# An RWKV/HGRN layer on one core: RWKV in units of four head pairs, HGRN in units of two heads, attention scores of 256 queries a bank

## The chip, the cores and the metric

The kernel runs on one core of a Trainium2 chip. The metric is the device time of one execution in microseconds (us). A core has TensorE (PE, with its weight loads as PEld), VectorE (DVE), ScalarE (ACT), GpSimd (POOL), SyncE (SP, which here issues the transfers) and 16 DMA engines. Matrix products land in the eight banks of PSUM (`bank` in the profile), all else lies in SBUF.

## The reference

One layer works on 1024 prompt tokens and 32 sample tokens of width 1024; the sample has its own recurrent states and memory.

```python
n = rmsnorm(x, norm_mix); p = n @ w_in                 # 2048 HGRN + 1792 RWKV columns
x += concat(hgrn2(p[:, :2048]), rwkv7(p[:, 2048:])) @ w_out
x += cross_attend(rmsnorm(x, norm_cross), mem_k, mem_v, w_cq, w_co)   # 4 heads of 256, 256 memories
n = rmsnorm(x, norm_ffn)
x += (silu(n @ w_ff1) * (n @ w_ff3)) @ w_ff2           # width 2816
y = rmsnorm(x, norm_final)
# hgrn2: 4 heads of 128, state S[k, v]
S = decay[:, None] * S + k_t[:, None] * v_t;  o_t = q_t @ S
# rwkv7: 8 heads of 64, state S[v, k]
sa = S @ (-kk_t)
S = S * w_t + outer(sa, kk_t * a_t) + outer(v_t, k_t); y_t = S @ r_t
```

The outputs are y for both, the last HGRN and RWKV states, the last projected RWKV row, and the memory's keys and values. Inputs and outputs are float32.

## The kernel before

Activations lie with their features on the partitions and the 1056 tokens along the free axis, in blocks of 352 or quarters of 264. A float32 product is made of three fp32r products (high x high, high x low, low x high): each weight tile of 1024 x 128 is loaded (`wr`), cast to its high part by ScalarE (`rw`) and split into its low part by VectorE (`rw<-wr,rw`), and a block of it is 24 dense matmuls (`gemm`, L881; the same in `fast`, L1283, and `memory_kv`, L994). Small products of the mixers go in plain float32, which PE runs as two records each.

The stages, by the profiled execution: mixers and input projection (0 to 708 us), keys and values of the memory (654 to 723), output projection (723 to 840), cross attention (708 to 1117), the two halves of the feed-forward (1079 to 1536 and 1536 to 1749), the last norm (to 1776).

`load_rows` (L905) loads nine tiles of x with 128 tokens (32 in the last), squares them on ScalarE, takes the root on GpSimd, scales by norm and gain on VectorE, transposes on PE and splits into high and low parts (ScalarE casts, VectorE subtracts). The gain comes as a broadcast transfer of 128 x 1024. `keep_rows` (L939) transposes each raw tile and stores it for the residual.

`mixers` (L1506) then writes the mixers' work. Projected tiles go to DRAM (`p_scratch`) and come back in the shape that a unit wants. `first` (L1609) projects r, k and v for the head pairs 0 and 1, six tiles of 128 columns, in the first block of 352 tokens and then in the others; the other tiles come as each consumer is written.

`rwkv(j)` (L1644) is called for the head pairs 0,1 and for 2,3. A unit is two pairs by 256 tokens, as eight chunks of 64 tokens, four units and one of 32 tokens for the sample. Its first half (kind `rw`) makes decays, keys, masked products of a chunk and the inverse of a triangular matrix. Its second half (kind `rc`) walks the chunks in order: a state step is the product `ps_b`, an addition, the product `ps_sa`, two copies, the product `ps_h` and the new state. Each of the three products is four matmuls of 64 columns (two pairs, two halves), and there are 17 steps for each call, 34 in all.

`hgrn(i)` (L1949) handles one head. A unit is 256 tokens of it in two groups of 128: exponentials and logarithms on ScalarE, a scan over blocks of 32 tokens, products of queries and keys with them, a masked 128 x 128 score for each group (`copy_predicated`), the state update, and the normed, gated output. There are four units and a sample unit for each head, 20 in all.

`attend` (L1108) scores 128 queries against 256 memories in a bank, takes maximum, exponential and sum, scales, transposes, splits, and multiplies with the values.

The order is not that of the code. Every operation is recorded as a node (L348) and all are issued at L392, so each row of the profile has that line. `plan` (L462) chooses the order by lists: it goes by each node's rank (the longest way to the end, moved by `START` and `NUDGE`, a table of numbers), by estimated costs (`price`, L229), by how many buffers of a kind are free (`FIFO`, L73), by how many units of a kind may be open, and by a charge for PE to change between forms of its array (`change`, L304). All engines then run their lists in order and wait for each other's semaphores.

## Time and profile before

| | |
|---|---|
| runs | 1792.44, 1788.71, 1786.61 us, median 1788.71 |
| profiled execution | 1785.72 us, its span 1783.9 |
| mean granted clock of TensorE | 0.997 |
| busy, share of the span | PE 98%, PEld 93%, DVE 73%, ACT 49%, POOL 25% |
| instructions | PE 15823, DVE 2743, ACT 2071, POOL 628 |
| the chain that ended last | PE 65%, DVE 8%, ACT 3%, DMA 2% |

A row of the timeline has the start, the duration, the engine, the line, the operation, what it writes and reads with its shape, how many operations the row joins, and in brackets the idle time before it and what ended it. A group of the page has busy time, mean ns of one and the idle time of the engine before them. A row of the table by stretches has the stretch, its length, busy time and count of PE, PEld, DVE, ACT and POOL, the clock granted, the DMA share and GB/s. `f`, `mb`, `r`, `rw`, `rs` and `wr` are kinds of SBUF memory, each shared by many tiles.

### The profile page before, as it was taken

The numbers are of one execution on the slowest core, as the hardware profiler recorded it, in microseconds if no ns is written. First come the engines' busy times: TensorE is split into PE (matmuls) and PEld (weight loads), VectorE is DVE, ScalarE is ACT, GpSimd is POOL, SyncE is SP. The second block draws the span as 40 slices with busy tenths as digits, with TensorE's granted clock in tenths as the row PEclk, the third lists the DMA queues.
The fourth block names the chain that finished last, engine by engine and source line by source line (L and its number), as shares of the span: only waits on it lengthen the run. The fifth ranks groups of instructions, "written<-read, shape, count | busy, mean of one in ns | idle before, by whom it ended". The sixth has DMA issues, their size and how long they took to land.

```text
span 1783.9 us, 40074 instructions
## 1 busy us (share of the span) xinstructions
PE 1741.6 (98%) x15823; PEld 1666.1 (93%) x15823; DVE 1296.0 (73%) x2743; ACT 875.2 (49%) x2071; POOL 448.0 (25%) x628
## 2 busy tenths in 40 slices
PE   7999999999999999999999999999999999999998
PEld 6998988899888889999999999999999999999997
DVE  6467669857876887323755367998877778968997
ACT  5755557664657668432333356332333333653432
POOL 5000112321102314252000047323322223222321
PEclk9999999999999999999999999999999999999999
DMA  7733223242323148642121242133222244655522
GB/s 222 211 106 108 64 80 89 66 118 88 102 57 96 45 131 260 214 145 85 54 78 36 78 147 90 34 125 113 91 99 99 94 131 151 193 151 158 182 84 98
DMA packets 213900, 203.99 MB, mean 114 GB/s; under 512 B 19448, under 2 KB 201072, under 8 KB 213712
## 3 DMA queue, kind: packets, MB, share of 16 engines
q1 hardware_dynamic: 213712, 201.44, 36.4%
q8 instruction: 124, 2.03, 0.5%
q14 instruction: 64, 0.52, 0.1%
HBM read 140.64 MB, written 60.75 MB: 113 GB/s over the span
## 4 chain that ended last, share of the span: by engine, by line
PE 65%; DVE 8%; ACT 3%; DMA 2%; issue 1%; POOL 0%; SPq 0%; DVEq 0%; ACTq 0%
PE bank L392 65%; DVE f L392 3%; DVE mb L392 3%; ACT mb L392 2%; DVE rw L392 1%; DVE r L392 1%; ACT f L392 1%; SPq L392 0%; POOL f L392 0%; DMA f<-mix_scratch 0%; DMA p_scratch<-mb 0%; ACT rw L392 0%; DMA f<-in_w_cv_dram 0%; DMA out_dram<-f 0%; DMA mix_scratch<-f 0%
## 5 line engine op out<-in xcount | busy, mean ns | idle before, releaser
L392 PE MATMUL bank<-r,rw 128*128 128x264 f32 (+1 forms) x5928 | 894.6, 304 | 9.5 <-DVE rw L392 4.6
L392 PEld LDWEIGHTS bank<-r,rw 128*128 128x128 f32 x5928 | 840.1, 188 | 17.9 <-DVE rw L392 6.1
L392 PE MATMUL bank<-mb,rw 128*128 128x264 f32 (+3 forms) x3672 | 514.7, 293 | 1.2 <-DVE f L392 0.6
L392 PEld LDWEIGHTS bank<-mb,rw 128*128 128x128 f32 x3672 | 485.7, 188 | 6.5 <-DVE f L392 1.4
L392 DVE TENSOR_TENSOR f<-bank,f 128x264 f32<-128x264 f32 (+5 forms) x466 | 207.7, 456 | 150.7 <-PE bank L392 135.8
L392 ACT CAST rw<-wr 128x1024 fp32r<-128x1024 f32 (+3 forms) x163 | 117.6, 728 | 192.2 <-PE bank L392 164.1
L392 POOL TENSOR_TENSOR f<-f 128x2 f32<-128x2 f32 (+8 forms) x170 | 104.2, 623 | 333.3 <-ACT f L392 261.6
L392 DVE TENSOR_TENSOR f<-f 128x264 f32<-128x264 f32 (+6 forms) x257 | 167.8, 671 | 18.7 <-ACT f L392 14.1
L392 ACT ACTIVATE f<-f 128x256 f32<-128x256 f32 (+6 forms) x275 | 119.9, 458 | 119.0 <-DVE f L392 74.4
L392 DVE TENSOR_TENSOR rw<-wr,rw 128x1024 fp32r<-128x1024 f32 (+3 forms) x163 | 143.2, 886 | 31.6 <-ACT rw L392 23.2
L392 PE MATMUL bank<-f 128*128 128x128 f32 (+15 forms) x1008 | 146.5, 287 | 2.8 <-DVE f L392 1.0
L392 ACT CAST rw<-r 128x512 fp32r<-128x512 f32 (+2 forms) x123 | 69.2, 564 | 118.7 <-PE bank L392 98.2
L392 PE MATMUL bank<-f,mb 128*128 128x64 f16 (+2 forms) x1969 | 110.0, 217 | 15.4 <-DMA mb<-in_x_prompt_dram 6.7
L392 PEld LDWEIGHTS bank<-f 128*128 128x128 f32 (+7 forms) x1008 | 105.4, 159 | 19.1 <-issue 4.3
L392 ACT COPY mb<-bank 128x512 f32<-128x512 f32 (+5 forms) x175 | 77.1, 453 | 75.1 <-PE bank L392 58.2
L392 DVE TENSOR_TENSOR rw<-r,rw 128x512 fp32r<-128x512 f32 (+2 forms) x123 | 86.9, 708 | 31.0 <-ACT rw L392 30.1
L392 PE MATMUL bank<-mb 64*64 64x64 f32 (+6 forms) x2060 | 94.8, 225 | 3.5 <-DVE mb L392 3.2
L392 ACT COPY f<-bank 128x264 f32<-128x264 f32 (+5 forms) x197 | 67.3, 361 | 61.5 <-PE bank L392 57.5
L392 PEld LDWEIGHTS bank<-mb 64*64 64x64 f32 (+3 forms) x1852 | 69.9, 138 | 15.2 <-issue 4.7
L392 ACT ACTIVATE mb<-mb 128x512 f32<-128x512 f32 (+8 forms) x141 | 75.6, 551 | 10.5 <-POOL mb L392 5.8
L392 PEld LDWEIGHTS bank<-f,mb 64*64 64x64 f32 (+4 forms) x1021 | 53.1, 140 | 22.2 <-issue 9.3
L392 POOL TENSOR_TENSOR r<-r 128x512 f32<-128x512 f32 (+2 forms) x37 | 53.4, 1450 | 79.9 <-DMA r<-in_w_ff_dram 45.9
(166 smaller groups left out, 1829.3 us busy)
## 6 DMA issues: line engine op xcount, KB each, us to landing
wr<-in_w_in_dram SPq DMA_DIRECT2D x36, 512.0 KB
p_scratch<-mb SPq DMA_DIRECT2D x87, 176.0 KB
wr<-in_w_ff_dram SPq DMA_DIRECT2D x26, 512.0 KB
r<-in_w_ff_dram SPq DMA_DIRECT2D x26, 512.0 KB
f<-h_scratch SPq DMA_DIRECT2D x33, 264.0 KB
f<-p_scratch SPq DMA_DIRECT2D x66, 128.0 KB
r<-h_scratch SPq DMA_DIRECT2D x31, 264.0 KB
h_scratch<-f SPq DMA_DIRECT2D x19, 396.0 KB
```

The lines of the kernel that those rows point to most:

```text
L392: getattr(eng, method)(*args, **kw)
```

## The change

- RWKV is one pass: a unit is all four head pairs by 128 tokens, still eight chunks of 64. There are eight units and a sample unit, 17 state steps, each product with eight matmuls. Products with the small weights (`psw`, `psa`, the gate) have 128 columns, and v is transposed earlier. `first` projects all twelve r, k and v tiles for the first block and then for the others.
- HGRN takes two heads at once, 512 columns, in ten units. Operands are written in place of their sources, the clamp goes from GpSimd to VectorE, one `copy_predicated` masks four groups. All HGRN units stand behind RWKV in the code.
- Attention scores, maxima, sums and transposes of 256 queries share a bank, and the products with the values take the term with the low part of the probabilities last.
- `gemm`, `fast` and `memory_kv` issue, for every four tiles of depth, four products high x high, four with the low activations and four with the low weights.
- `load_rows` begins with an activation of one element, loads the gain as one row of 4 KB and spreads it by two matmuls with ones; raw tiles are kept for the residual only behind the tile at token 256.
- The planner knows when within a node an operand is needed (`lag`), charges turns between dense and other work (`TURN`), counts two more GpSimd operations as sharing VectorE's port, and has fewer buffers for `pr` and `ph`, four for `cg`, and another table.

```diff
-START, NUDGE = (68066, 0.2), ((35, 7642, 3), (55, 8846, 3), ...
+START, NUDGE = (94419, 0.1), ((40, 8857, 0.3), (50, 3388, 3), ...
+TURN = 0.035, -0.06, 0.085, 0.0
-FIFO = {..., "pr": 6, "pl": 2, "ph": 12, ...}
+FIFO = {..., "pr": 3, "pl": 2, "ph": 4, ..., "cg": 4}
...
+def lag(n, s):
+    return wait(n, s) - (s.preds[n] or 0.0)
...
# gemm
-                nc.tensor.matmul(ps, lhsT=hi[:, k], rhs=ah, start=i == 0, stop=False)
-                nc.tensor.matmul(ps, lhsT=hi[:, k], rhs=al, start=False, stop=False)
-                nc.tensor.matmul(ps, lhsT=lo[:, k], rhs=ah, start=False, stop=i == nk - 1)
+                for part, w in ((0, hi), (1, hi), (0, lo)):
+                    for k in ks[i:i + CUT]:
+                        nc.tensor.matmul(ps, lhsT=w[:, k], rhs=act(k, part, t0, n), ...
...
# load_rows
+        S.activation(warm[:, 0:1], warm[:, 1:2], AF.Square)
+        row = self.tmp([128, D], "grow1")[0:1]
+        nc.sync.dma_start(row, self.i["norm_mix"]).soon = SOON
-        nc.sync.dma_start(gain, self.i["norm_mix"].to_broadcast([128, D])).soon = SOON
+            PE.matmul(ps, lhsT=self.ones[0:1], rhs=row[:, 512 * kg:512 * kg + 512], start=True, stop=True)
+            V.tensor_copy(gain[:, 512 * kg:512 * kg + 512], ps)
...
# attend
-                    ps = self.psm.tile([128, 256], F32, tag="m", name="ps_sc")
+                ps = self.psm.tile([128, 2, 256], F32, tag="m", name="ps_sc")
-                    V.tensor_reduce(st[:m, 0:1], ps[:m], mybir.AxisListType.X, ALU.max)
+                V.tensor_reduce(st[:m, 0, :ng], ps[:m, :ng], mybir.AxisListType.X, ALU.max)
-                    terms = [(a, x, y) for a in range(2) for x, y in (((0, 0), (0, 1), (1, 0)) ...
+                    terms = [(a, x, y) for x, y in (((0, 0), (1, 0), (0, 1)) ... for a in range(2)]
...
# mixers, first
-        for j in (0, 2):
-            self.rwkv(j)
-            for i in (j, j + 1):
-                self.hgrn(i)
+        self.rwkv()
+        for i in (0, 2):
+            self.hgrn(i)
-            for tile in (0, 1, 4, 5, 8, 9):
+            for tile in range(12):
                 self.rw_proj(tile, bias=0.0, blocks=blocks)
...
# rwkv
-        for s in range(5):
-            m, c0 = (4, 256 * s) if s < 4 else (1, TP)
+        for s in range(9):
+            m, c0 = (2, 128 * s) if s < 8 else (1, TP)
             for c in range(m):
-                ps = self.psc.tile([128, 2, 64], F32, tag="c", name="ps_b")
-                for a in range(2):
+                ps = self.psc.tile([128, 4, 64], F32, tag="c", name="ps_b")
+                for a in range(4):
...
# hgrn
-            G.tensor_scalar(e, f, -80.0, 3e38, ALU.max, ALU.min)
+            V.tensor_scalar(e, f, -80.0, 3e38, ALU.max, ALU.min)
-            qg, kg, kd, qt = self.u("hqg", n), self.u("hkg", n), self.u("hkd", n), self.u("hqt", n)
+            qg, kg, kd, qt = e1, bm, k, e0
-                V.copy_predicated(am[:m, :m], self.mask_h[:m, :m], psh[:m, g, :m])
+            V.copy_predicated(am[:m, :, :m], self.mask_h[:m, :m].unsqueeze(1).to_broadcast([m, ng, m]), psh[:m, :ng, :m])
```

Three places in the order, on the engines that wait or are waited for there. The names end in a number for the memory they lie in. ScalarE at the start of the program, before: the table load, squares of x (`128x1025`), the copies of raw x that `keep_rows` stores, and the high parts of x (`CAST`).

```order
L392 ACT_TABLE_LOAD
L392 ACTIVATE mb_87,f_0_71<-mb_87 128x1025
L392 COPY mb_87<-bank_58 128x512
L392 COPY mb_87<-bank_59 128x512
L392 ACTIVATE mb_87,f_0_71<-mb_87 128x1025
L392 COPY mb_87<-bank_60 128x512
L392 ACTIVATE mb_87,f_0_71<-mb_87 128x1025
L392 CAST r_0_79<-bank_62 128x4x128
```

And now:

```order
L401 ACT_TABLE_LOAD
L401 ACTIVATE f_0_71<-f_0_71 1x1
L401 ACTIVATE mb_87,f_0_71<-mb_87 128x1025 x3
L401 CAST r_0_79<-bank_60 128x4x128
L401 CAST r_0_79<-bank_61 128x4x128
L401 CAST rw_83<-wr_75 128x1024
```

The table load has an operation of its own that needs no x, and the three copies ahead of the first cast stand behind it.

PE in a state step of RWKV, before: a unit's `ps_b`, then that of another unit, the first masked product of that other one, transposes of HGRN units, the `ps_sa` of the first, dense work, and its `ps_h`.

```order
L392 MATMUL bank_58<-mb_87 64x64 x4
L392 MATMUL bank_62<-mb_87 64x64 x4
L392 MATMUL bank_60<-mb_87 64x64 x4
L392 MATMUL bank_59<-f_0_71 128x32
L392 MATMUL bank_61<-f_0_71 128x128 x2
L392 MATMUL bank_63<-f_0_71,mb_87 64x64 x4
L392 MATMUL bank_64<-f_0_71 128x128 x2
L392 MATMUL bank_58<-r_0_79,rw_83 128x352 x12
...
L392 MATMUL bank_63<-mb_87 64x64 x4
```

And now: `ps_sa` of a step, an HGRN transpose, dense work, `ps_h`, dense work and the scores of an HGRN unit, and `ps_b` of the next step.

```order
L401 MATMUL bank_58<-f_0_71,mb_87 64x64 x8
L401 MATMUL bank_64<-f_0_71,mb_87 128x128 x4
L401 MATMUL bank_60<-r_0_79,rw_83 128x352 x12
L401 MATMUL bank_63<-mb_87 64x64 x8
L401 MATMUL bank_62<-r_0_79,rw_83 128x352 x12
L401 MATMUL bank_65<-rs_91 128x512 x2
L401 MATMUL bank_61<-mb_87 128x128 x4
L401 MATMUL bank_61<-mb_87 32x32 x8
L401 MATMUL bank_61<-f_0_71 64x64 x4
L401 MATMUL bank_58<-mb_87 64x64 x8
```

A piece is eight matmuls where it was four, and serves four head pairs where it served two.

VectorE in an HGRN unit, before: products over all and over part of the blocks, a split for RWKV between, and two masks.

```order
L392 TENSOR_TENSOR f_0_71<-f_0_71 128x256
L392 TENSOR_TENSOR f_0_71<-f_0_71 128x2x96 x2
L392 TENSOR_TENSOR f_0_71<-f_0_71 128x2x32 x2
L392 TENSOR_TENSOR rs_91<-mb_87,rs_91 128x512
L392 TENSOR_TENSOR f_0_71<-f_0_71 128x256 x2
...
L392 COPY_PREDICATED f_0_71<-f_0_71,bank_59 128x128 x2
```

And now, for two heads:

```order
L401 TENSOR_TENSOR mb_87<-mb_87 128x512
L401 TENSOR_TENSOR mb_87<-mb_87 128x4x96
L401 TENSOR_TENSOR mb_87<-bank_62,f_0_71 128x512
L401 TENSOR_TENSOR mb_87<-mb_87 128x512
...
L401 TENSOR_TENSOR mb_87<-mb_87 128x4x32
...
L401 COPY_PREDICATED f_0_71<-f_0_71,bank_60 128x512
```

Each works on twice the width, and there is one in place of two or four. Masks of 128 columns stand before at twelve of 36 places within the first half of the mixers' rows on VectorE (the first at row 203 of some 1030); now the eight masks of 512 stand at rows 344 to 757 of 776.

More of the change, by code (lines that the diff above doesn't have):

```diff
@@ L490, in plan @@
         for n in reversed(nodes):
-            n.path = n.cost + n.late + max((s.path + wait(n, s) for s in succs[n]), default=0.0)
+            n.path = n.cost + n.late + max((s.path + lag(n, s) for s in succs[n]), default=0.0)
         for n in nodes:
@@ L929, in load_rows @@
                 S.copy(hs, ps[:, :, :n])
+                last = nc.nodes[-1]
                 V.tensor_tensor(ls, ps[:, :, :n], hs.bitcast(F32), ALU.subtract)
-            self.keep_rows(raw, n, t0)
+            held.append((raw, n, t0))
+            if t0 >= 256:
+                gate = gate or last
+                for one in held:
+                    self.keep_rows(*one, gate)
+                held = []
         self.xact = lambda k, lo, t0, n: x[lo][k // 4][:, k % 4, t0:t0 + n]
@@ new lines, in attend @@
+                        PE.matmul(ps[:m, g], lhsT=qs[a][:, tg:tg + m], rhs=kt[:, a], start=a == 0, stop=a == 1)
+                pr = self.ap.tile([128, 2, 256], F32, tag="pr", name="pr")
+                nc.claim([*prt, pr])
+                st = self.ap.tile([128, 4, 2], F32, tag="st", name="st")
+                V.tensor_reduce(st[:m, 0, :ng], ps[:m, :ng], mybir.AxisListType.X, ALU.max)
+                V.tensor_scalar(st[:m, 1, :ng], st[:m, 0, :ng], -1.0 / 16, None, ALU.mult)
+                for g in range(ng):
+                    S.activation(pr[:m, g], ps[:m, g], AF.Exp, bias=st[:m, 1, g:g + 1], scale=1.0 / 16, accum_out=st[:m, 2, g:g + 1])
@@ new lines, in attend @@
+                V.reciprocal(st[:m, 3, :ng], st[:m, 2, :ng])
+                for g in range(ng):
+                    V.tensor_scalar(pr[:m, g], pr[:m, g], st[:m, 3, g:g + 1], None, ALU.mult)
+                ps = self.psm.tile([128, 2, 256], F32, tag="m", name="ps_pt")
+                for g in range(ng):
+                    for a in range(2):
+                        PE.transpose(ps[:, a, 128 * g:128 * g + m], pr[:m, g, 128 * a:128 * a + 128], self.ident[:m, :m])
+                if s < 4:
+                    self.split(*prt, ps)
+                else:
+                    V.tensor_copy(prt[0][:, :, :m], ps[:, :, :m])
@@ L1183, in cross @@
                 self.late = nc.nodes[-1]
-            self.gemm(w, act, KD, self.operands(m, sq), blocks=[(TQ * q, TQ) for q in range(4)])
+            self.gemm(w, act, KD, self.operands(m, sq), blocks=[(TQ * q, TQ) for q in range(4)], tag="cg")
         nc.bias = 25.0
@@ L1510, in mixers @@
         for n in first:
-            if n.bufs and not any(b in (self.ident.buf, self.nhalf.buf) for b in n.bufs):
+            if n.bufs and not any(b in (self.ident.buf, self.nhalf.buf, self.ones.buf) for b in n.bufs):
                 n.preds[self.ready] = None
@@ L1943, in scratch_h @@
     def scratch_h(self):
[L1944 to L1947 removed]
+        self.ah = self.mc.tile([128, 4, 128], F32, name="ah")
+        self.nc.gpsimd.memset(self.ah, 0.0)
     def hgrn(self, i):
@@ L2039, in hgrn @@
-            psh = self.psm.tile([128, 2, 128], F32, tag="m", name="ps_ha")
-            for g in range(ng):
-                gl = slice(128 * g, 128 * g + m)
-                PE.matmul(psh[:m, g, :m], lhsT=kg[:, gl], rhs=qg[:, gl], start=True, stop=True)
+                sts = [self.s("hst") for h in range(2)]
+                for h in range(2):
+                    nc.sync.dma_start(sts[h], self.i["state_hgrn"][0, 0, i + h])
+            sg = self.v("hsg", N)
+            self.sigmoid(sg, p)
+            for h in range(2):
+                V.scalar_tensor_tensor(of(sg, h), of(p, h), self.P("hn", i + h), of(sg, h), ALU.mult, ALU.mult)
@@ L2043, in hgrn @@
+            psh = self.psm.tile([128, 4, 128], F32, tag="m", name="ps_ha")
+            for g in range(ng):
+                PE.matmul(psh[:m, g, :m], lhsT=kg[:, at_group(g)], rhs=qg[:, at_group(g)], start=True, stop=True)
             if m == 128:
```

343 lines of the change are left out of this document (166 added, 177 removed).

## The prediction

> **What bounds the kernel now.** I read the page's first part, then the waits of PE, the groups by shape, the table by stretches, and the timeline at three places.
>
> ```profile
> span 1783.9 us, 40074 instructions
> PE 1741.6 (98%) x15823; PEld 1666.1 (93%) x15823; DVE 1296.0 (73%) x2743; ACT 875.2 (49%) x2071; POOL 448.0 (25%) x628
> ```
>
> TensorE (PE) works 1741.6 of 1783.9 us. So 42.3 us is all that better overlap can ever give back, and anything larger has to come out of the 1741.6. What PE waits for, with total, times and longest:
>
> ```profile
> PE bank L392 <- DVE f L392: 8.2, 14, 2.7
> PE bank L392 <- DMA mb<-in_x_prompt_dram: 6.7, 1, 6.7
> PE bank L392 <- DVE rw L392: 6.4, 9, 1.6
> PE bank L392 <- DVE mb L392: 4.6, 11, 0.8
> PE bank L392 <- DVE r L392: 4.1, 4, 1.1
> ```
>
> The second row is the first load and the last row belongs to the start, where x is split. VectorE's f, rw and mb, 19.2 us together, are the waits of the rest: state updates, weight splits, masks. No single one is long.
>
> ```profile
> L392 PE MATMUL bank<-r,rw 128*128 128x352 f32 x2736 | 472.6, 327 | 5.2 <-DVE rw L392 3.1 <-DVE r L392 1.1 <-DVE f L392 0.7
> L392 PE MATMUL bank<-r,rw 128*128 128x264 f32 x3192 | 422.0, 285 | 4.3 <-DVE f L392 2.7 <-DVE rw L392 1.4
> L392 PE MATMUL bank<-mb,rw 128*128 128x264 f32 x2952 | 389.4, 285 | 1.2 <-DVE f L392 0.6 <-ACT rw L392 0.4
> L392 PE MATMUL bank<-mb,rw 128*128 128x352 f32 x576 | 100.4, 328 | 0.0
> ```
>
> These dense fp32r products hold 1384.5 us. Their numbers and widths, 3312 of 352 columns and 6144 of 264, are the same in both programs, so only what lies between them can move.
>
> **Part 1: fewer small matmuls between dense ones.** A state step of RWKV is a few 64x64 products between dense runs:
>
> ```profile
> 105.31 1.15 PE L392 MATMUL bank<-mb 64*64 64x64 f32 x32
> 106.39 0.41 PE L392 MATMUL bank<-f,mb 128*128 128x64 f16 x8
> ...
> 143.25 2.09 PE L392 MATMUL bank<-r,rw 128*128 128x352 f32 x12
> 145.27 0.45 PE L392 MATMUL bank<-f,mb 64*64 64x64 f32 x8
> 145.65 2.19 PE L392 MATMUL bank<-r,rw 128*128 128x352 f32 x12
> 147.67 0.63 PE L392 MATMUL bank<-rs 128*128 128x512 f32 x2
> 66.58 21.08 PE L392 MATMUL bank<-r,rw 128*128 128x352 f32 x130 [1.59 <-DVE rw L392]
> ```
>
> From start to start, 32 small ones (each matmul in float32 is two records) take 106.39-105.31 = 1.08 us, 0.034 each. In the long run at 66.58 a dense one takes 21.08/130 = 0.162. The twelve at 143.25 take 145.27-143.25 = 2.02, where 12 x 0.162 = 1.94: going into the small form costs 0.08. The eight at 145.27 take 0.38, where 8 x 0.034 = 0.27: coming out costs 0.11. So a change between forms of the array costs about 0.10 us. The old order of PE has 345 such changes, the new one 209: 17 state steps of eight products for 34 of four, each with three pieces (17 x 3 x 2 = 102), and HGRN and the rest give the other 34. 136 x 0.10 = -13.6. There are 46 more PE instructions (13,947 for 13,901: two matmuls for the gain, finer gate products), about +1. Part of what is saved becomes more breaks by 128x128 products, so the least I allow is -10. I take **-12** (-10 to -14). The inner order of the dense products (four high by high, then the mixed ones) costs nothing: the rows above with r and with mb as the weights' partner, which reuse operands differently, have 285 and 285, 327 and 328 ns.
>
> **Part 2: the start.**
>
> ```profile
> 6.65 1.28 ACT L392 ACT_TABLE_LOAD   x1 [6.65 <-DMA mb<-in_x_prompt_dram]
> 9.00 1.05 ACT L392 COPY mb<-bank 128x512 f32<-128x512 f32 x2
> ...
> 19.80 3.30 PE L392 MATMUL bank<-r,rw 128*128 128x352 f32 x12 [1.14 <-DVE r L392]
> ...
> 6.00:10.00 4.00, 3.29 (x16) 3.27 (x16) 0.16 (x1) 3.34 (x6) 0.55 (x1) 1.00 1.03 403
> 10.00:14.00 4.00, 3.18 (x28) 2.83 (x27) 3.27 (x4) 4.00 (x9) 1.85 (x4) 1.00 1.08 388
> 14.00:18.00 4.00, 2.15 (x17) 1.49 (x14) 4.00 (x6) 4.00 (x9) 3.46 (x12) 1.00 0.55 225
> 18.00:22.00 4.00, 2.85 (x13) 2.62 (x14) 3.75 (x5) 4.00 (x10) 3.67 (x8) 0.81 0.62 170
> 22.00:26.00 4.00, 4.00 (x24) 3.93 (x24) 3.24 (x8) 2.81 (x6) 3.69 (x11) 0.76 0.04 10
> ```
>
> Behind the length the columns are PE, weight load, VectorE, ScalarE and GpSimd busy, then the clock, DMA share and GB/s. ScalarE is busy in every microsecond from 10 to 22, and the first dense run at 19.80 waits for it through the splits. The change takes from ahead of that run the table load (1.28), 512 KB of broadcast gain at some 400 GB/s (1.3), and three copies of 0.53 (1.6): 4.2. It puts two copies of 512 columns on VectorE, which is itself full from 14 to 18. I take **-3.5** (0 to -6).
>
> The clock rows say 0.81 and 0.76: 4 x 0.19 + 4 x 0.24 = 1.7 us of full rate is lost there. The Trainium skill ("TensorE: Matmul & The Clock Gate", What's actually happening) has half rate follow an idle window of 3413 ns; the length agrees (2 x 1.7 = 3.4 us), the idleness less, since PE worked 2.15 of the 4 us before. By that rule a denser start would spare these 1.7 us as well; I count nothing for it.
>
> **Part 3: weights for the first block.** All twelve r, k and v tiles are now projected for the first 352 tokens before the others, where six were.
>
> ```profile
> 78.81 1.05 ACT L392 CAST rw<-wr 128x1024 fp32r<-128x1024 f32 x1 [2.51 <-DMA wr<-in_w_in_dram]
> ...
> 82.98 1.05 ACT L392 CAST rw<-wr 128x1024 fp32r<-128x1024 f32 x1 [2.52 <-DMA wr<-in_w_in_dram]
> ```
>
> Loads and splits give a tile every 82.98-78.81 = 4.17 us; PE uses one in 24 x 0.162 = 3.89. Six more such tiles owe 6 x 0.28 = 1.7 us. Nothing if the two buffers run ahead, two waits of 2.5 if they don't: **+1.5** (0 to +5).
>
> **Part 4: the waits of 19.2 us.** With half as many state steps, more dense work stands between a step's products. Counted in the two orders at the prices above, nine in ten of the pieces that follow a step's first product have at least 6.5 us of PE work between, where it was 1.4. Scores of 256 queries a bank mean one softmax for two, and the term that needs the low halves comes last. Against this every update is twice as wide. Bounds are 0 to -6, a third of the waits; I take **-3**.
>
> **Part 5: HGRN gathers in the second half.** In the old order, 12 of the 36 masks of HGRN stand in the first half of the mixers' VectorE rows; in the new one, the first full unit's mask is at row 344 of 776. A two-head unit asks of VectorE:
>
> ```profile
> L392 DVE TENSOR_TENSOR mb<-mb 128x512 f32<-128x512 f32 x24 | 16.5, 689 | 7.8 <-ACT mb L392 4.6 <-issue 2.8
> L392 DVE SCALAR_TENSOR_TENSOR mb<-mb,f 128x256 f32<-128x256 f32 x54 | 24.9, 495 | 1.7 <-ACT mb L392 1.3
> L392 DVE TENSOR_TENSOR f<-f 128x256 f32<-128x256 f32 x52 | 21.5, 423 | 5.0 <-ACT f L392 4.4
> 63.41 1.24 DVE L392 TENSOR_TENSOR_SCAN mb<-f,mb 128x520 f32<-128x520 f32 x1 [5.88 <-issue]
> 98.02 0.74 DVE L392 COPY_PREDICATED mb<-f,bank 128x512 f32<-128x512 uint32 x1
> ```
>
> Eight operations of 512 at 0.69 (the clamp among them, from GpSimd), four of 256 at 0.50, a scan of 1.24, a mask of 0.74, and some 2.0 for the four state updates and the partial products: 5.5 + 2.0 + 1.2 + 0.7 + 2.0 = 11.4 us, eight units 91. Counted so, HGRN's work on VectorE is 46 us in the old stretch from 400 to 640, and 76 in the new one: 30 more. The old stretch, with a dense one for comparison:
>
> ```profile
> 280.00:340.00 60.00, 58.38 (x795) 52.14 (x796) 53.90 (x170) 41.06 (x128) 17.80 (x50) 1.00 0.23 65
> ...
> 400.00:460.00 60.00, 58.14 (x683) 53.03 (x682) 43.69 (x100) 36.17 (x107) 8.36 (x18) 0.97 0.32 96
> 460.00:520.00 60.00, 57.62 (x839) 50.96 (x837) 50.31 (x119) 34.00 (x69) 8.87 (x20) 1.00 0.24 67
> 520.00:580.00 60.00, 58.07 (x672) 51.74 (x668) 43.54 (x102) 38.24 (x89) 12.25 (x23) 1.00 0.32 91
> 580.00:640.00 60.00, 59.20 (x818) 52.70 (x817) 51.23 (x162) 37.01 (x114) 16.99 (x49) 1.00 0.25 79
> ...
> 1640.00:1743.00 103.00, 101.77 (x818) 100.23 (x817) 100.33 (x237) 41.53 (x92) 30.41 (x35) 1.00 0.41 128
> ```
>
> From 400 to 640 VectorE works 188.8 of 240 us and PE loses 7.0. Adding 30 gives 219, a load of 0.91. Counting the new order's operations there by shape instead gives about 234 us beside 226 of PE work, 1.03. At 0.90 (280 to 340) PE loses 1.6 in 60, no more than elsewhere; at 0.97 (1640 to 1743) it loses 1.2 in 103. So a load of 0.91 costs nothing. At 234 us and 0.97, the stretch takes 241, 15 over its PE work, 8 more than the 7 lost now. At 0.90 it takes 260, +27. A gain isn't excluded, since there are fewer instructions: -3. Nearest is the row of 0.97: **+6** (-3 to +27). Over all mixers VectorE's work hardly changes (527 to 525 us by the same count); it's the place that counts.
>
> **Sum.** -12 - 3.5 + 1.5 - 3 + 6 = -11.0. The profiled execution took 1785.72 us itself (span 1783.9, 1.8 around it): 1774.7. The median shown, 1788.71, is 3.0 above that execution: **1778 us**.
>
> **Rivals.**
> *VectorE becomes the bound of the mixers' second half*, and the kernel is slower. Its place is the stretch above, its price up to +27 in place of +6: 1799. It decides where VectorE can't be kept above 234/250 = 0.94 there: then the stretch costs 24 over its PE work, 17 over the 7 of today, and the sum comes to 1789; at 0.92 it's 254, +21, 1793, and below that it's slower. For it: one engine serves two heads' chain at once. Against it: the row at 0.97, and that only the count by shape reaches 1.03. 1793 to 1799.
>
> *Wider operations lengthen the waits*: PE waits for f and mb in the rows above 12.8 us. If those waits grew as an operation does from 256 to 512 columns, 689/423 = 1.63, they'd cost +8.1 in place of Part 4's -3: 1789, no change. For it: VectorE has 27% idle, and its waits are waits on a chain. Against it: half the steps are gone, and the wide ones have more dense work beside them. The Trainium skill ("Perfetto Trace Analysis", Optimizing Scalar/DVE Operations) speaks for this rival: grouping helps if the engine is saturated, and where an unsaturated engine causes bubbles elsewhere, smaller instructions may let work complete sooner. The 0.79 of the stretch says unsaturated, so by this rule the change works against itself there; no run so far shows the wide form.
>
> *The waits fall too*: Part 5 at -3 and Part 4 at -6 give 1766. For it: ScalarE has 1827 instructions for 1963, GpSimd 506 for 624, VectorE 2523 for 2743. Against it: nothing shortens the stretch of Part 5. 1760 to 1769.
>
> *The switch price is hidden*, that is, PE would have waited anyway: only Part 1 goes, 1790. Against it: PE waits 2% of the time, so few switches stand in a wait.
>
> **How the numbers follow.** Forecast 0.50; waits fall too 0.18; wider operations or hidden switches 0.20; VectorE the bound 0.12. Faster or slower means over 0.3% off 1788.7, about what a measurement of this kernel tells from no change: under 1783.3 or over 1794.1. The first two cases are faster, 0.68; the third is the same; of the fourth nearly all is slower. The range of the forecast itself is 1770 to 1783. For 8 in 10, down to the low case with a few us more from the start and up to where the third ends: 1760 to 1792.
>
> **What would show it.** Part 1: PE's busy time falls by 8 to 14 us, to about 1730, and the dense groups keep their means. Part 2: the first twelve dense products start near 16 us in place of 19.80. Part 3: casts that wait for weights between 45 and 110 us. Part 4: the waits for f, rw and mb under 17 us outside the second half. Part 5: VectorE over 0.9 busy from 400 to 630 and PE losing 10 to 15 us there. PE's busy time unchanged would make Part 1 wrong; over 25 us lost in that stretch would make the forecast wrong.

## The result and the profile after

The changed kernel took 1766.18 us (median of four executions, 1764.76 to 1772.58) against 1788.88 for the kernel before: a ratio of 0.9878, interval 0.9849 to 0.9907, 22.7 us less. The forecast was 1778 us, 10.7 less: the direction was right and the time lies in the wider range (1760 to 1792), but the gain is more than twice the forecast and below the narrow one (1770 to 1783). Later comparisons of the same kernel gave 0.9908 (0.9893 to 0.9923) and 0.9887 (0.9874 to 0.9901), 17.0 and 19.8 us less. All twelve executions of it lie between 1764.8 and 1772.6, with a median of 1768.9. The gain is near 20 us, a little under twice the forecast.

The profiled execution was the longest of its four, 1772.58 us. The first lines of its page, and what PE waited for (total, times, longest):

```profile
span 1770.7 us, 39634 instructions
PE 1727.0 (98%) x15915; PEld 1667.0 (94%) x15915; DVE 1280.4 (72%) x2523; ACT 858.8 (49%) x1933; POOL 418.9 (24%) x510
...
PE bank L401 <- DVE mb L401: 10.4, 13, 2.6
PE bank L401 <- ACT f L401: 6.5, 5, 2.1
PE bank L401 <- DVE f L401: 4.7, 7, 1.7
PE bank L401 <- ACT mb L401: 3.3, 6, 1.4
PE bank L401 <- DVE rw L401: 3.1, 2, 1.5
PE bank L401 <- DMA mb<-in_norm_mix_dram: 2.3, 1, 2.3
```

PE's busy time fell by 14.6 us, and it still fills 98% of the span. The waits did not shrink, they changed hands: f and rw fell from 14.6 to 7.8, mb grew from 4.6 to 10.4, and ScalarE, 2.7 before, holds PE up for 9.8 in the rows above.

By stretches, with the columns as before (PE, weight load, VectorE, ScalarE, GpSimd, clock, DMA share, GB/s). First the kernel before, in the stretches not yet shown:

```profile
0.00:40.00 40.00, 28.30 (x179) 26.48 (x180) 26.88 (x53) 25.02 (x46) 26.52 (x77) 0.96 0.74 235
40.00:100.00 60.00, 58.02 (x457) 55.88 (x457) 31.12 (x59) 41.63 (x91) 4.04 (x10) 1.00 0.61 175
640.00:700.00 60.00, 58.49 (x583) 54.37 (x584) 47.77 (x133) 49.79 (x148) 21.75 (x44) 1.00 0.65 192
```

And the changed kernel:

```profile
0.00:40.00 40.00, 32.33 (x192) 28.35 (x192) 28.08 (x56) 24.15 (x44) 28.02 (x78) 1.00 0.66 215
40.00:100.00 60.00, 59.67 (x393) 58.70 (x391) 29.80 (x53) 41.04 (x93) 3.04 (x7) 1.00 0.69 201
400.00:460.00 60.00, 58.37 (x796) 53.92 (x793) 49.37 (x109) 40.81 (x83) 6.13 (x13) 1.00 0.41 115
460.00:520.00 60.00, 56.94 (x772) 52.27 (x769) 55.30 (x122) 42.61 (x106) 18.98 (x31) 0.97 0.29 79
520.00:580.00 60.00, 58.30 (x792) 52.85 (x792) 50.76 (x121) 36.86 (x90) 11.31 (x26) 0.97 0.20 56
580.00:640.00 60.00, 54.40 (x733) 49.68 (x732) 44.54 (x134) 41.91 (x119) 5.75 (x18) 0.94 0.45 135
640.00:700.00 60.00, 54.07 (x476) 50.71 (x476) 44.39 (x90) 43.72 (x116) 17.15 (x33) 0.96 0.63 191
```

PE is busy 4.0 us more in the start and 1.7 more in the next stretch. But 3.7 of the 4.0 are the products that spread the gain, which the kernel before doesn't have:

```profile
2.33 3.75 PE L401 MATMUL bank<-mb,f 1*128 1x512 f32 x4 [2.33 <-DMA mb<-in_norm_mix_dram]
8.71 4.41 PE L401 MATMUL bank<-f,mb 128*128 128x128 f32 x20 [2.63 <-DVE mb L401]
...
15.94 2.18 PE L401 MATMUL bank<-r,rw 128*128 128x352 f32 x12
```

From 400 to 700 PE loses 17.9 us where it lost 8.5. The clock is low there too, 0.94 to 0.97 from 460 on. There PE ran at half rate for 3.4 us at a time. The execution has seven such pieces ahead of its tail, six of them in these stretches; the kernel before had two. So busy time hides two things, and I split it. "Lost to half rate" is half of the busy time that lies in half-rate pieces; the rest is PE's work at full rate. "Idle" is all of PE's idle time up to its last product, the first wait included.

| profiled execution | PE busy | lost to half rate | work at full rate | idle |
|---|---|---|---|---|
| before | 1741.6 | 3.4 | 1738.2 | 34.7 |
| changed | 1727.0 | 11.7 | 1715.4 | 36.0 |
| difference | -14.6 | +8.3 | -22.8 | +1.3 |

-22.8 + 8.3 + 1.3 is -13.2, the difference of the two spans. The work fell by far more than I counted, and a cost that I didn't count took part of it back. Without the gain's products, the work that both kernels share fell by 26.5 us; those products ran in a wait.

### The profile page after: what moved, and what is told of

It reads as the page before. It is cut to its first block, busy times and chain, and to the rows that moved or that the text cites. A ratio compares the mean times of both kernels' runs of the same rounds, so it can differ in the third digit from the quotient of the medians.

```text
span 1770.7 us, 39634 instructions
## 1 busy us (share of the span) xinstructions
PE 1727.0 (98%) x15915; PEld 1667.0 (94%) x15915; DVE 1280.4 (72%) x2523; ACT 858.8 (49%) x1933; POOL 418.9 (24%) x510
## 4 chain that ended last, share of the span: by engine, by line
PE 76%; DVE 12%; ACT 4%; DMA 3%; issue 2%; POOL 1%; SPq 0%; DVEq 0%; ACTq 0%; POOLq 0%
PE bank L401 76%; DVE mb L401 5%; DVE f L401 3%; ACT mb L401 3%; DVE rw L401 1%; DVE r L401 1%; POOL f L401 1%; ACT f L401 1%; DVE rs L401 1%; DMA mb<-p_scratch 1%; DMA f<-mix_scratch 0%; ACT rw L401 0%; DMA mb<-in_x_prompt_dram 0%; ACT r L401 0%; DMA f<-x_scratch 0%
## 5 line engine op out<-in xcount | busy, mean ns | idle before, releaser
L401 DVE TENSOR_TENSOR f<-f 128x264 f32<-128x264 f32 (+5 forms) x207 | 175.4, 862 | 11.2 <-ACT f L401 8.9
L401 POOL TENSOR_TENSOR f<-f 128x264 f32<-128x264 f32 (+8 forms) x113 | 82.9, 740 | 373.0 <-ACT f L401 300.0
L401 PE MATMUL bank<-f,mb 128*128 128x64 f16 (+4 forms) x2166 | 122.7, 216 | 12.9 <-DVE mb L401 6.0
L401 ACT ACTIVATE f<-f 128x264 f32<-128x264 f32 (+7 forms) x153 | 80.2, 539 | 99.2 <-DVE f L401 54.1
L401 PE MATMUL bank<-f 128*128 128x128 f32 (+11 forms) x1024 | 116.8, 278 | 3.5 <-ACT f L401 2.0
L401 ACT ACTIVATE mb<-mb 128x512 f32<-128x512 f32 (+5 forms) x161 | 98.7, 627 | 24.5 <-DVE mb L401 11.2
L401 PE MATMUL bank<-mb 64*64 64x64 f32 (+5 forms) x2260 | 103.0, 233 | 3.8 <-DVE mb L401 3.6
L401 PEld LDWEIGHTS bank<-f 128*128 128x128 f32 (+6 forms) x1024 | 90.9, 163 | 15.2 <-issue 4.4
L401 PEld LDWEIGHTS bank<-mb 64*64 64x64 f32 (+4 forms) x2260 | 91.2, 144 | 14.1 <-DVE mb L401 4.6
L401 ACT ACTIVATE mb<-bank,f 128x128 f32<-128x128 f32 (+6 forms) x187 | 68.5, 422 | 27.6 <-PE bank L401 21.6
```

The source lines that it names most:

```text
L401: getattr(eng, method)(*args, **kw)
```

## The experiments

The runs that are compared below as one group ran on one chip, with the kernel before beside them. "The changed order" means that all instructions keep their places and only the named ones differ.

### The changed kernel again, and PE's gaps filled

The first was the changed kernel, run again in two groups (no edit):

> The changed kernel once more, unaltered. Its profiled execution took 1772.58 us with a mean granted clock of 0.992, its other three 1764.8 to 1766.8 with 0.994 to 0.996. Theory A: the profiled one was a long one, because PE ran at half rate in seven stretches of 3.4 us (before: two), and the executions differ by how many such stretches they have. Then the times here lie at 1762 to 1770, the gain over the kernel before at 20 to 24 us, and 0.001 of mean clock goes with about 1.8 us. Rival B: the profiled one is typical and the three were lucky: median 1770 or more, a gain of 13 to 17.

> The changed kernel unaltered, beside the others of this call on one chip: 1764 to 1773, at 0.001 more mean clock some 1.5 us less.

They gave 1770.47 (1768.68 to 1772.53) beside 1787.48 before, and 1768.11 (1765.05 to 1770.52) beside 1787.89. The first median answers to rival B. But the clock does go with the time: of the twelve executions, the six with a mean clock of 0.994 or more average 1766.4 us, the six below 1770.9. That is 4.5 us for 0.0027, or 1.7 for 0.001. So much of what differs from execution to execution is how long PE is put on half rate, and the first four happened to hold three with a high clock.

The second filled gaps. `FILL` names places in PE's order and how many products stand there:

```diff
+                        if out not in self.used:
+                            ps, ident = self.banks[out.at][:, 0:128], self.full.real()
+                            for _ in range(FILL.get(self.count, 0)):
+                                eng.matmul(ps, lhsT=ident, rhs=ident, start=True, stop=True)
```

> The changed kernel in its own order, with 37 idle 128x128 products put on PE in 11 of the places where it waited over 0.5 us between 480 and 1160 us; they write to the bank that the waiting product is about to overwrite, so the result is unchanged. Where PE would have waited anyway they cost nothing. Theory A (half rate follows PE's idle gaps): the mean clock rises to 0.996 or above, and the time falls by 3 to 8 us to 1759 to 1763. Rival B (half rate comes from elsewhere, or costs nothing in the end): the clock stays near 0.994 and the time stays or grows by up to 37 x 0.24 = 9 us.

1770.87 us (1769.38 to 1771.73), beside 1770.47 for the changed kernel in the same group. The last two stretches of the mixers, the changed kernel's own rows first:

```profile
580.00:640.00 60.00, 55.16 (x743) 50.54 (x743) 45.26 (x136) 43.42 (x122) 6.18 (x19) 0.94 0.45 137
640.00:700.00 60.00, 55.43 (x471) 52.30 (x470) 42.96 (x86) 42.79 (x114) 16.50 (x33) 0.92 0.65 197
```

With the gaps filled:

```profile
580.00:640.00 60.00, 57.44 (x796) 52.44 (x792) 47.19 (x139) 44.97 (x125) 8.46 (x22) 1.00 0.48 143
640.00:700.00 60.00, 56.53 (x487) 53.90 (x488) 42.93 (x84) 42.56 (x114) 15.35 (x30) 0.97 0.64 195
```

The clock rose as theory A said (over the execution 0.992 to 0.996), so half rate does follow PE's gaps. The loss to it fell from 11.5 to 5.1 us. But the filler was 9.5 us of work and displaced only 2.8 us of idle time: the time stayed, as in rival B. A filler that waits for the bank itself runs only when the gap is over; at the 1156 us gap it waited 1.8 us and then took 2.7 of its own.

### The price of a change between forms

Two kernels in the changed order put idle small products ahead of the first product of a bank in the first half of the feed-forward, the second of them eight at every second place (`% 2` and `range(8)`):

```diff
+                    if node.phase == 4 and node.dense and kw.get("start"):
+                        self.starts += 1
+                        if self.starts % 1 == 0:
+                            ps, small = args[0].real()[0:64, 0:64], self.small.real()
+                            for _ in range(4):
+                                eng.matmul(ps, lhsT=small, rhs=small, start=True, stop=True)
```

> The changed kernel in its own order; each of the some 154 first products of a bank in the first half of the feed-forward has four idle 64x64 products ahead of it, in the bank that it overwrites. PE is 98% busy there. 616 small products cost 616 x 2 x 0.030 = 37 us, and 308 changes between forms 308 x p. My prediction: p = 0.10 or a little under, 31, together +68. The traces of the two kernels compared: p = 0.114, 35, +72. Alone this decides little; with the next run it gives p.

> As the run before, with eight small products at every second place: the same 616 products and half the changes, 154. If a change costs 0.085, as the -12 taken for 141 changes amounts to, this is 13 us faster than the run with fours; at 0.10, 15; at 0.114, 18. If PE's changes are hidden behind its waits, the difference is under 5.

There were 184 such places, not 154, so 736 products (1472 records) in each. With fours it took 1915.4 us (1913.7 to 1918.8), with eights 1889.1 (1888.2 to 1889.5). Equal products, 184 changes less, 26.3 us: 0.143 us a change. In the profiled executions the work at full rate differs by 32.7 us (1865.0 and 1832.3), 0.178 a change; the kernel with eights lost 4.7 more to half rate and idled some 3 more. The sum of each run alone was far off (+145 and +119 us, where +68 was expected of the first), because these products follow each other at 0.063 us, where those of a state step take 0.034. A likely reason is that mine all sit in one quarter of the array, and a state step uses two in turn; no run tested it. Fours first:

```profile
1251.89 6.02 PE L408 MATMUL bank<-mb,rw 128*128 128x264 f32 x48
1257.84 0.67 PE L405 MATMUL bank<-f 64*64 64x64 f32 x8
1258.44 1.73 PE L408 MATMUL bank<-mb,rw 128*128 128x264 f32 x12
```

And eights:

```profile
1249.78 6.02 PE L408 MATMUL bank<-mb,rw 128*128 128x264 f32 x48
1255.73 1.14 PE L405 MATMUL bank<-f 64*64 64x64 f32 x16
1256.80 1.72 PE L408 MATMUL bank<-mb,rw 128*128 128x264 f32 x12
```

Eight records last 0.60 us from start to start, sixteen 1.07: the eight more cost 0.47, 0.059 each, and 0.13 is left over for coming out. The two traces of the mixers, taken apart by which form follows which, hold 333 changes before and 192 after at 0.118 and 0.119 us beyond the usual spacing: 39.3 and 22.8 us. That includes places where PE also waited for a moment; without them the mean is near 0.11 and the median 0.10. So my pair of rows was typical of the change itself.

What it leaves out stands one product later. In the kernel with fours, 169 pieces of dense products follow small ones, and the second product starts 0.227 us behind the first, while all others follow at 0.122: a return costs 0.10 once more. In the mixers of the kernel before it is 0.266 for 0.163, at 51 returns to a run of 352 columns, and the changed kernel has 28. The planner has such a charge, 0.1 (`HIDE`) beside 0.095 for the change (`SWITCH`); my sum has only the change. By whole kernels a change costs 0.14 to 0.18, by my sum 0.085. The Trainium skill has the drain in words ("TensorEngine Tiling (Array Packing)", Key Properties): changing the tiling mode, not just the tile, drains the engine. That page gives no figure.

### Structure or table

Four kernels of one group have an empty table, so that the order comes from the planner's rules alone. A table made for one structure means nothing for another.

```diff
-START, NUDGE = (94419, 0.1), ((40, 8857, 0.3), ...
+START, NUDGE = (0, 0.0), ()
```

> The changed kernel with START and NUDGE empty: its order by the planner's rules and costs alone. It is the base for the next three runs, whose structure differs and for which a table of numbers made for another structure means nothing. The order has 212 changes between forms of the array (with the table 209). Theory S (structure: fewer changes make the gain, and the table only trims waits): PE's busy time stays within 2 us of the changed kernel's, the time grows by 5 to 15 us through waits, 1775 to 1785. Theory T (the table makes the gain): 1787 or more.

The next takes `rwkv` of the kernel before (two pairs by 256 tokens, with its six input buffers), and calls it for each pair of pairs, with `hgrn` between:

```diff
-        self.rwkv()
-        self.enter(None)
-        for i in (0, 2):
-            self.hgrn(i)
+        for j in (0, 2):
+            self.rwkv(j)
+            self.enter(None)
+            self.hgrn(j)
```

> As the run before, empty table, but RWKV in the old units: two head pairs by 256 tokens, 34 state steps (the first projections and everything else as changed). 330 changes between forms in place of 212. Theory S: 118 changes at 0.114 (from the traces) to 0.143 us (from the inserted products) are 13 to 17 us of PE work more, and the time is longer by that much, 1790 to 1800. At the 0.085 that I reckoned with, 10. Rival W (the change gains by waits, through fewer and wider VectorE instructions): PE work within 5 us, and the difference in PE's idle time.

The third takes `hgrn` and `scratch_h` of the kernel before, with twelve input buffers:

```diff
-        for i in (0, 2):
+        for i in range(4):
             self.hgrn(i)
...
-FIFO = {..., "ph": 4, ...}
+FIFO = {..., "ph": 12, ...}
```

> As the base, empty table, but HGRN one head at a time: 20 units of 256 columns, operands in their own buffers, 130 VectorE and 108 ScalarE instructions more. 236 changes between forms in place of 212: 24 x 0.114 to 0.143 = 3 us. Theory S: 3 us longer than the base, give or take 4 for another order. My Part 5 (paired units fill VectorE and cost 6 us of waits): shorter by up to 3. Rival W: longer by 8 or more, from waits.

And the fourth takes the scores and the order of terms of the kernel before in `attend`:

```diff
-                ps = self.psm.tile([128, 2, 256], F32, tag="m", name="ps_sc")
+                    ps = self.psm.tile([128, 256], F32, tag="m", name="ps_sc")
...
-                    terms = [(a, x, y) for x, y in (((0, 0), (1, 0), (0, 1)) ... for a in range(2)]
+                    terms = [(a, x, y) for a in range(2) for x, y in (((0, 0), (0, 1), (1, 0)) ...]
```

> As the base, empty table, but attention scores of 128 queries a bank and the old order of the terms. 64 VectorE instructions more, PE's changes the same (211). Theory S: no difference beyond 3 us, since PE waited 2.3 us in all in that stage before. Rival W: longer by 4 to 8.

Later, on another chip, the kernel before had its own table emptied:

> The kernel before with START and NUDGE empty. Its order has 358 changes between forms, the changed kernel with an empty table 212. Theory S: the structure's gain shows without tables too: 146 changes at 0.12 are 18 us, with the rest of what the changed kernel saves on PE 20 to 27, so this run lies that much over the changed kernel with an empty table (1791), at 1811 to 1818, and the old table was worth as much as the new one, about 22. Theory T: it lies within 8 of 1791, and the new table makes the gain.

| empty table | time | against changed | work at full rate | idle | lost to half rate |
|---|---|---|---|---|---|
| changed kernel | 1791.0 | | 1720.7 | 48.4 | 13.3 |
| old RWKV units | 1819.6 | +28.6 | 1743.9 | 48.4 | 13.6 |
| old HGRN units | 1817.0 | +25.9 | 1725.6 | 64.2 | 17.6 |
| old attention | 1809.0 | +18.0 | 1720.6 | 59.5 | 25.2 |
| kernel before | 1837.7 | +46.7 | 1743.9 | 59.0 | 25.5 |

(Times are medians; work, idle time and loss are those of the profiled executions, so their differences need not add up to the time's.) The page of the changed kernel with an empty table, and of the one with old RWKV units:

```profile
span 1789.7 us, 39815 instructions
PE 1734.0 (97%) x15915; PEld 1671.3 (93%) x15915; DVE 1268.8 (71%) x2523; ACT 865.3 (48%) x1937; POOL 408.7 (23%) x510
```

```profile
span 1813.2 us, 39702 instructions
PE 1757.5 (97%) x15827; PEld 1677.0 (92%) x15827; DVE 1273.6 (70%) x2558; ACT 866.8 (48%) x1954; POOL 392.1 (22%) x502
```

With fewer records, PE works 23 us longer in the old units, and idles the same. So RWKV's units carry most of the saved work: 23.2 us, where the shared work of the two tuned kernels differs by 26.5. Taken apart, 113 changes more make 14 of it; the rest, 9, lies between products of the same form, 3.5 of it at 34 returns more to dense runs of 352 columns. That is theory S, but larger than its 13 to 17 us of work, and the time grew by 5 us more than the work.

The other two parts look different. Old HGRN units add 4.9 us of work and 15.8 of idle time, old attention adds no work and 11.1 of idle time. By their size both results are rival W's, and my Part 5 had paired HGRN units cost 6 us. But another order moves waits by chance too, and the end of the kernel shows how much. Behind 1100 us, the base, old HGRN and old attention:

```profile
1100.00:1782.00 682.00, 673.35 (x5440) 668.07 (x5440) 558.88 (x999) 260.31 (x526) 204.70 (x165) 0.99 0.37 119
1100.00:1807.00 707.00, 689.22 (x5542) 683.44 (x5541) 576.94 (x1013) 268.79 (x552) 208.69 (x173) 0.99 0.36 114
1100.00:1804.00 704.00, 686.34 (x5494) 680.63 (x5494) 573.83 (x1006) 264.24 (x537) 203.85 (x170) 0.98 0.36 115
```

Nearly all that PE runs there is the feed-forward, which neither edit touches, and PE idles 8.7, 17.8 and 17.7 us. So 9 us of each difference arise where neither edit acts. That leaves 7 us of waits for old HGRN units and 2 for old attention, less than those 9. The three differences also add up to 72.5 us, where all old parts together cost 46.7. So neither the 18 and 26 us nor their signs are prices of the units; one order of each was measured.

The changed kernel without its table, at 1791, lies where theory T put it, over the 1785 that S allowed: its PE work is 5.3 us above the tuned one's and its idle time 12.4. So the new table is worth some 20 to 23 us. But T falls with the kernel before, which without its own table takes 1837.7 us, not within 8 of 1791; the old table was worth 48. Structure against structure the change gains 46.7 us without tables (S had 20 to 27), with them about 20: the old table had already won back more than half of that difference.

### The start

In the changed order, the gain comes as the broadcast transfer again and the early activation is left out:

```diff
+                    if node.phase == 0 and ("ps_gain" in names or (method == "activation" and "warm" in names)):
+                        continue
+                    if method == "dma_start" and "grow1" in names:
+                        eng.dma_start(self.gain[0].real(), self.gain[1])
+                        continue
...
+        nc.gain = gain, self.i["norm_mix"].to_broadcast([128, D])
```

> The changed kernel in its own order, but the gain of the first norm comes as the broadcast transfer of 512 KB again (no row, no two matmuls with ones, no two copies), and the early one-element activation is left out, so that ScalarE's table load waits for the first square again. By Part 2 of the prediction: 1.28 for the table load and 1.3 for the transfer, 2.6 us slower (1 to 4) than the changed kernel, 1770.5 in its last run. Rival: the start is bound elsewhere (VectorE's splits), and the difference is under 1.

> The gain as a broadcast transfer and the late table load once more, now beside the changed kernel on one chip. In the first such run PE lost 6.1 us more in the first 40 us and had 2.3 us less work, but executions between 1767 and 1776 hid the rest. Part 2: 1 to 4 us slower at the same mean clock. Rival: no difference.

The first gave 1771.35 us, with executions from 1767.1 at a clock of 0.996 to 1775.9 at 0.990; no changed kernel ran beside it, so it decides nothing. The second gave 1772.68 (1767.57 to 1774.70) beside 1768.11, +4.6 with much overlap. In the means it is +3.7, and the mean clock is lower by 0.0016, which by the 1.7 us above makes some 2.6 of it. The first 40 us, the changed kernel and then this one:

```profile
0.00:40.00 40.00, 33.10 (x197) 28.88 (x197) 28.08 (x56) 24.37 (x45) 28.15 (x78) 1.00 0.66 215
```

```profile
0.00:40.00 40.00, 26.33 (x172) 24.88 (x173) 26.69 (x54) 23.87 (x43) 27.95 (x76) 1.00 0.70 228
```

PE does 6.8 us less in them, 3.7 of which are the left-out products themselves, which ran while nothing else could. So without the two parts PE is 3.0 us behind at 40 us; Part 2 priced them at 2.6. At the end nothing is left of it: over the whole execution idle time is 3.7 us longer and work 3.5 shorter. The early lead is shown, a gain of the whole kernel isn't.

### The inner order of the dense products

```diff
+                if node.dense and len(calls) == 12:
+                    calls = [calls[4 * part + k] for k in range(4) for part in range(3)]
```

> The changed kernel in its own order of nodes, but within each node of twelve dense products the old inner order again: high x high, high x low, low x high for one tile of depth after the other. My Part 1 gave the inner order nothing. By that, PE's work at full rate stays at 1715 us and the time at 1770; since the low parts are wanted earlier, waits may cost 0 to 3. Rival D: the means of dense products in the two traces (122.4 and 122.1 ns, 123.4 and 122.7, 166.5 and 165.0) are the inner order's, and PE's work grows by 3 to 5 us, the time by as much.

1772.0 us (1770.7 to 1776.4) beside 1768.1: +3.9. PE's work is 1716.0 against 1715.6, so my reading that the order costs PE nothing stands, and rival D falls. But in the profiled executions idle time grew from 34.4 to 38.4. In the new order the first low weights are wanted as the ninth product and not as the third, six products or 1.0 us later, and the low activations as the fifth and not the second. That goes with 4 us of waits. I had given the edit nothing at all.

### Load or chain in the second half

Weight splits of VectorE outside the units, in the changed order, on a quarter of their columns:

```diff
+                    if node.eng == "vector" and node.phase < 2 and self.count > 2800 and args[0].buf.name == "wlo":
+                        args = [a[:, 0:a.shape[1] // 4] if isinstance(a, View) else a for a in args]
```

> The changed kernel in its own order; 26 of VectorE's splits of 1024-column weight tiles, those behind some 340 us in the mixers and the memory's keys, work on the first quarter alone (the low parts of the rest are left out). It takes 26 x 0.8 = 21 us from VectorE between 340 and 700 us, none of it inside an HGRN or RWKV unit. Load theory (Part 5: VectorE is too full there): PE's idle time between 400 and 700, 16.1 us in the last run of the changed kernel, falls by 6 or more, the time by 5 to 9. Chain theory (PE waits for the steps of units one behind the other while VectorE too waits): it falls by less than 3.

> 26 weight splits on a quarter of their columns once more (the low parts of the rest left out), beside the changed kernel on one chip. Load theory: 5 to 9 us less. Chain theory: under 3 less. The first run had 6.9 less than the changed kernel of another call, with idle time down by 2.9 and 3.9 less lost to half rate.

And operations within the HGRN units on half:

```diff
+                        if method in ("tensor_tensor_scan", "copy_predicated") or late and ...
+                            args = [a[:, 0:a.shape[1] // 2] if isinstance(a, View) else a for a in args]
```

> The changed kernel in its own order; in the HGRN units seven of VectorE's operations behind the logarithms (the scan, five products, the mask) work on the first half of their columns alone, the other half being left as it is. About 2.3 us from each of eight units, 18 us in all, on the chain of the units. Load theory: as the run before, in proportion: idle time falls by 5 or more. Chain theory: it falls by 3 to 8, clearly more than in the run before. If neither run moves it by 3, the waits come from another engine or from transfers.

The lighter splits gave 1763.58 in one group and 1764.54 (1762.64 to 1769.46) in that of the changed kernel at 1768.11: 3.6 less, between the two expectations. Idle time fell by 2.9 us, from 34.4 to 31.5. From 400 to 700, the changed kernel and then the lighter one:

```profile
400.00:700.00 300.00, 283.16 (x3557) 260.55 (x3556) 243.72 (x571) 206.89 (x513) 57.23 (x121) 0.97 0.40 118
```

```profile
400.00:700.00 300.00, 285.80 (x3608) 263.67 (x3607) 230.74 (x573) 207.99 (x516) 55.88 (x121) 0.98 0.42 121
```

VectorE has 13 us less to do there and PE loses 2.6 us less of 16.8. Shorter HGRN operations, some 17 us of VectorE's time on the chain, gave 1760.24, 3.3 less than the first lighter run beside it, though they took less from VectorE. But that is not a matter of waits: from 400 to 700 PE lost 14.1 us, as with the second lighter run (14.2), and of the difference between the profiled executions 2.6 us are half rate, 1.3 work and 0.4 idle time. The chain theory wanted clearly less idle time than the lighter splits leave. So either edit spares some 3 us of PE's idle time, load and chain can't be told apart by them, and most of the 16.8 us is neither. One gap of the changed kernel shows a third kind:

```profile
609.92 0.70 PE L401 MATMUL bank<-rs 128*128 128x512 f32 x2
610.47 1.95 ACT L401 ACTIVATE mb<-mb 128x512 f32<-128x512 f32 x3 [2.47 <-DMA mb<-p_scratch]
611.27 0.43 DVE L401 TENSOR_SCALAR mb<-mb 128x512 f32<-128x512 f32 x1 [1.20 <-DMA mb<-p_scratch]
612.33 0.63 ACT L401 CAST f<-bank 128x256 f16<-128x256 f32 x2
612.73 0.28 PE L401 MATMUL bank<-f,mb 128*128 128x64 f16 x4 [2.11 <-ACT f L401]
```

An HGRN unit's input is late. ScalarE waits 2.47 us for it, with RWKV's cast behind in its list, and PE waits 2.11 us for the cast. It's PE's longest wait for ScalarE in that profile, and VectorE stands idle for 1.2 us too. The input buffers were cut from twelve to four of twice the width; whether more of them would cure it wasn't tried.

## Why the prediction was right or wrong

**The step that failed is the term of Part 1, mis-sized.** It put PE's work at -12 us (-10 to -14); it fell by 22.8. The count was near: 141 changes fewer for 136. The price was not. At 0.118 us each they come to 16.5, where I had 0.10 and then took off 1.6 for more matmuls and breaks. Even that is short, because a price read at the change misses the second product behind it; at the 0.143 to 0.178 of the two whole kernels, 141 changes are 20 to 25 us (an estimate: other small products stood there).

Not all of the 22.8 is explained. In the mixers work fell by 18.0, 21.8 without the gain's products. The changes are 16.5 of it, later returns to dense runs of 352 columns 2.4, and some 3 us stay open. Another 4.8 us lie behind the mixers. With the old inner order the stages there took some 2 us more (and the mixers 1.7 less), so it explains less than half of them; the rest stays open. One term was mis-sized the other way: I gave all additional products about +1, and the gain's alone take 3.7, though in a wait.

**Part 2 came true in the start, and not in the time.** -3.5 forecast; the first dense run began at 15.94 in place of 19.80. But of 4.0 us more PE time in the first 40, 3.7 are the gain's products. At full rate and without them PE did 28.6 us of work there for 26.6, and a half-rate piece at 20.5 us, which only the kernel before had, is 1.7 of these 2.0. Where a profiled execution of the changed kernel has such a piece, at 25 us, it is 26.5 to 26.9, no more than before. In the run without two of the three parts it is 26.3, for 29.4 of the changed kernel beside it, neither with such a piece.

**Part 3 had the wrong sign.** +1.5 forecast; from 40 to 100 us PE lost 0.3 in place of 2.0. Three casts still waited 1.1 to 3.6 us for weights (at 73.5, 76.3 and 88.5), but PE had enough to do meanwhile.

**Part 4, -3, came true in size alone.** Outside 400 to 700 us the waits for f, rw and mb fell from 12.3 to 8.7 us, inside they grew from 6.9 to 9.5. But its reasons aren't shown. The inner order, to which I gave nothing, goes with 4 us of waits in its own run; no run took the longer stretches between the products of a state step away by themselves.

**Part 5 had the size and not the reason, by luck.** +6 forecast within -3 to +27; from 400 to 640, the stretch that it named, PE lost 12.0 us for 7.0, and to 700 it lost 9.4 more. But VectorE works 200 of those 240 us, 0.83, not the 0.91 to 1.03 that I counted, and where PE loses most, from 580 to 700, it works 0.74. The rival "VectorE becomes the bound" is refuted by those rows and by the lighter splits. What made the waits grow stays open beyond the one late input above; with old units, in another order, they weren't fewer.

**Not in the sum: half rate.** I noted 1.7 us of it at the start and counted nothing later. It cost 8.3 us more in the profiled execution, and by the mean clock (0.991 to 0.996) how often it falls makes most of the 8 us between one execution of the changed kernel and another. The Trainium skill has this rule ("TensorE: Matmul & The Clock Gate", What's actually happening): an idle window of 3413 ns brings half rate. The length agrees, and filled gaps brought fewer such pieces. But a whole window of idle time isn't needed. In the 3.4 us ahead of each of the seven pieces (the two that follow each other at 695 us count once) PE idled 1.0 to 2.1 us. The first of them begins at 501.0:

```profile
498.50 2.00 PE L401 MATMUL bank<-mb 64*128 64x64 f32 x30 [1.00 <-DVE mb L401]
...
502.55 1.22 PE L401 MATMUL bank<-rs 128*128 128x512 f32 x2
...
507.86 0.70 PE L401 MATMUL bank<-rs 128*128 128x512 f32 x2
```

Behind one gap of 1.00 us a pair of products takes 1.22 us, and a pair of the same form 0.70 five us later.

**The offset.** I added 3.0 us from the profiled execution to the median. For the changed kernel the profiled one was 6.4 above its median. From profiled execution to profiled execution the sum is -11.0 against -13.1. That they are near is luck: -22.8 of work, +8.3 of half rate and +1.3 of idle time stand against -12 of work and +1.0 of waits.

**The rivals.** "The waits fall too", 1766 us, has the time by chance: PE's idle time grew by 1.3 us. "Wider operations lengthen the waits" is not borne out: the waits for f and mb went from 12.8 to 15.1 us, where it had +8.1, and with old, narrow units PE idled no less. That wide units by themselves spare waits isn't shown either. "The switch price is hidden" is refuted: with PE 97 to 98% busy, 184 changes fewer showed as 26.3 us of time.

## What to carry to other kernels

Where one engine is 98% busy, price a change of form by all that it does to the engine, the products behind it included, and best by two kernels that differ in nothing else; a pair of rows shows only a part. Making each visit to a small form serve twice the work was worth 23 us of PE's work here, while all of PE's idle time was 35. A finely searched order can hide half of a structure's cost, so compare structures with the search off on both sides, and look where the difference lies: two of three such differences lay in good part in a stage that the edit hadn't touched. Judge a change of this size against several executions, with the granted clock beside each.

## What the runs showed that I had not expected

- Filling PE's gaps raised the mean clock from 0.992 to 0.996 and gained nothing: 6.4 us less lost to half rate, 9.5 us of filler.
- 64x64 products that all sit in one quarter of the array followed each other after 0.063 us, those of the state steps, in two quarters by turns, after 0.034.
- Behind small products, the second dense product starts 0.10 us late (0.227 for 0.122 us at 264 columns, 0.266 for 0.163 at 352), besides the 0.10 at the change itself.
- The order of twelve dense products within a node changes PE's work by 0.4 us (1716.0 and 1715.6) and its waits by 4.
